# Three seven-product pairs, and pairs with adding DMA, in two recurrent input groups and the first half of an output projection

## The chip, the core and the metric

The kernel runs on one core of a Trainium2 chip. The metric is the device time of one execution in microseconds; the kernel before has a median of 1131.99 us in 3 runs (1131.68 to 1132.94). All times below are microseconds from the start of the profiled span unless marked otherwise. TensorE is called PE, VectorE DVE, ScalarE ACT, GpSimd POOL and SyncE SP, as in the profile.

## The reference

One residual block on 256 tokens of 2048 features, in float32. An input projection feeds an attention half (8 heads) and a recurrent half (8 heads, HGRN2 in chunks of 64); both go through one output projection, and a gated feed-forward follows.

```python
h = rmsnorm(x, norm1_gain[l])
proj = h @ w_in[l]            # q_a k_a v_a | q_r f_r i_r g_r, 1024 columns each
...
attn = rmsnorm(chunk_band_attention(q_a, k_a, v_a, rel_bias[l]), attn_out_gain[l])
rec = hgrn2_mixer(q_r, f_r, i_r, g_r, lb_all[l], grn_norm_gain[l])
# f = lb + (1-lb)*sigmoid(f_raw); k = 1-f; chunkwise recurrence with state
# o = rmsnorm(o) * gain * silu(g_raw)
x = x + concatenate([attn, rec]) @ w_out[l]
ff = silu(h2 @ w_gate[l]) * (h2 @ w_up[l])   # h2 = rmsnorm(x, norm2_gain)
x = x + ff @ w_down[l]
return rmsnorm(x, final_gain)
```

## The kernel before, in words

**Numbers in halves.** Every float32 factor is split into a high part that the array takes whole and a low remainder: ACT copies the high part (a tile named wh, L89) and DVE subtracts it from the raw weights to give the low part (wl, L90). A product is then three matmuls: hi x hi, hi x lo, lo x hi (L336 in the groups that the change touches, L151 and L153 for the transposed projections).

**Groups and pairs.** The columns are worked in groups of 1024 (a `Group`), the 2048-deep contraction in eight pairs of 256 rows. The weights of one pair are one raw tile of 128 x 2048 elements (1 MB), which SP loads (raw, L86) into a ring of three buffers. A pair is one of three kinds. A **d** pair runs 24 matmuls of 128x512 into four accumulators c00, c01, c10, c11; ACT makes two copies of 128x1024 and DVE two splits. An **s** pair forms 2 x 2 blocks as seven products (Strassen's scheme in Winograd's form): 21 matmuls into m1, m5, m6, m7 and three of the c accumulators; for it DVE also makes differences of weight blocks (ta at L385, tb at L386 and L387) and splits those, and the token side needs sums over blocks, made ahead by `row_sums` (tiles wsa and wsb). After the last s pair of a group the products are spread over the outputs. An **a** pair runs 24 matmuls but leaves DVE out: ACT writes the negated high part into a tile named low (L355), POOL issues an adding DMA that reads the same weights from memory a second time and adds them there (L356), and what remains is the low part. `begin` loads the raw of an a pair ahead, `lower` makes half of its low, and `prepare_begun` the high copies; its matmuls are ordered so that those that use low come last. Before, a pairs stand in the second half of the output projection and in the feed-forward.

**What sets the order.** Each engine has an in-order list, made by a scheduler from the program; some instructions are pinned in program order. `run_groups` prepares the next pair while one runs. For an a pair, `begin` and the first `lower` are called in front of the preparation of the pair before it. Between the pairs a number of pieces of the recurrence are taken from a queue (`ticks`), and the last pair of each group is held, so that its matmuls are run by output block together with the next to last.

**Buffers that the steps touch.** The pool of high copies (wh) has four buffers of 128x1024, so that a copy for a pair waits until PE has finished with one of four copies before. The ring of raw has three.

**The stages.** Attention inputs and heads run up to about 197.5; then the group for the recurrent values ("i0", called the value group here), 197.5 to 240; the second pair of transposed recurrent projections, to 291; the gate group ("g0") from 291, with the recurrence of the second four heads woven in; the first half of the output projection (`wout[0]`) from about 338, the second half (`wout[1]`) from about 384; then the feed-forward.

Of the kernel before, what the change touches and what calls it, by code (L numbers as in the profile page):

```python
# [16 lines left out]
P = 128  # L17
S = 256
# [3 lines left out]
W = 512  # L22
# [23 lines left out]
def hybrid_block(ctx: ExitStack, tc: tile.TileContext, x, xT, w_in, w_out, w_gu, w_down,  # L46
                 bias, gains, lbnd, fgain, out):
    nc = tc.nc
# [33 lines left out]
    def dma(o, i):  # L82
        with ExitStack() as st:
            if prev:
                st.enter_context(tc.issue_after(prev[-1]))
            prev.append(nc.sync.dma_start(o, i).ins)  # L86

    def split(hi, lo, src):
        nc.scalar.activation(hi, src, AF.Copy)  # L89
        nc.vector.tensor_tensor(lo, src, hi.bitcast(F32), ALU.subtract)  # L90
# [18 lines left out]
    queue = []  # L109
# [7 lines left out]
    def drain():  # L117
        while queue:
            queue.pop(0)()
# [170 lines left out]
    def row_sums(dst, hi, lo, in_order=False):  # L290
        n = hi.shape[1] // 2
        a = dn.tile([P, 2, 2, S], F32, tag="ta", name="a")[:, 0:n]
        sm = dn.tile([P, 4, 2, P], F32, tag="tb", name="sm")[:, :, 0:n]
        first = nc.vector.tensor_tensor(a, hi.rearrange("p (j k) t -> p j k t", k=2).bitcast(F32),
                                        lo.rearrange("p (j k) t -> p j k t", k=2).bitcast(F32), ALU.add)
        if in_order:
            tc.keep_in_program_order(first)
        a11, a12, a21, a22 = a[:, :, 0, 0:P], a[:, :, 1, 0:P], a[:, :, 0, P:S], a[:, :, 1, P:S]
        nc.vector.tensor_tensor(sm[:, 0], a21, a22, ALU.add)
        nc.vector.tensor_tensor(sm[:, 1], sm[:, 0], a11, ALU.subtract)  # L300
        nc.vector.tensor_tensor(sm[:, 2], a11, a21, ALU.subtract)
        nc.vector.tensor_tensor(sm[:, 3], a12, sm[:, 1], ALU.subtract)
        split(dst[:, 0], dst[:, 1], sm)
# [11 lines left out]
    class Group:  # L315
# [25 lines left out]
            return load_chunk(self.src, self.base + j).rearrange("p (b n) -> p b n", n=W)  # L341

        def begin(self, j):
            raw = own["low"].tile([P, 4, W], F32, name="rawa")
            flat, src = raw.rearrange("p b n -> p (b n)"), self.src[self.base + j]
            if self.src is w_out:
                tc.keep_in_program_order(nc.gpsimd.dma_start(out=flat, in_=src))
            else:
                dma(flat, src)
            self.begun = j, raw, []  # L350

        def lower(self, k):
            j, raw, low = self.begun
            wl = own["low"].tile([P, 2, W], F32R, tag="low", name="low", bufs=3)
            tc.keep_in_program_order(nc.scalar.activation(wl, raw[:, 2 * k:2 * k + 2], AF.Copy, scale=-1.0))  # L355
            nc.gpsimd.dma_start(out=wl.rearrange("p b n -> p (b n)"),  # L356
                                in_=self.src[self.base + j, :, 2 * k * W:2 * (k + 1) * W], accum_op=ALU.add)
            low.append(wl)

        def prepare_begun(self, j):  # L360
            (_, raw, low), self.begun = self.begun, None
            tiles = []
            for k in range(2):
                wh = wsp.tile([P, 2 * W], F32R, tag="wh", name="wh")
                nc.scalar.activation(wh, raw[:, 2 * k:2 * k + 2].rearrange("p b n -> p (b n)"), AF.Copy)
                tiles.append([(wh[:, i * W:(i + 1) * W], low[k][:, i]) for i in range(2)])
# [127 lines left out]
    def att_scores(box, hd, kq, qx, g):  # L494
        h = hd % 4
        sc = paux.tile([P, 384], F32, tag="aux", name="sc")
        nc.tensor.matmul(sc[:, 0:128], lhsT=kq[:, 1, h, :], rhs=kq[:, 0, h, :], start=True, stop=True)  # L497
        kh, kl, qh, ql = kx[:, g, 0, h, :], kx[:, g, 1, h, :], qx[:, 0, h, :], qx[:, 1, h, :]
        nc.tensor.matmul(sc[:, 128:384], lhsT=qh, rhs=kh, start=True, stop=False)
        nc.tensor.matmul(sc[:, 128:384], lhsT=qh, rhs=kl, start=False, stop=False)  # L500
        nc.tensor.matmul(sc[:, 128:384], lhsT=ql, rhs=kh, start=False, stop=True)
        s = box["s"] = abp.tile([P, 384], F32, tag="s", name="s", bufs=2)
        nc.vector.scalar_tensor_tensor(s, sc, ASCALE, G[:, hd, :], ALU.mult, ALU.add)
        nm_ = small.tile([P, 2], F32, tag="nmax", name="nmax")
        sm = small.tile([P, 2], F32, tag="asum", name="asum")
        for t, (a, b) in enumerate(halves):
            nc.vector.tensor_reduce(nm_[:, t:t + 1], s[:, a:b], AX.X, ALU.max, negate=True)
            nc.scalar.activation(s[:, a:b], s[:, a:b], AF.Exp, bias=nm_[:, t:t + 1],
                                 accum_out=sm[:, t:t + 1])
        nc.vector.reciprocal(sm, sm)  # L510
        for t, (a, b) in enumerate(halves):
            nc.vector.tensor_scalar(s[:, a:b], s[:, a:b], sm[:, t:t + 1], None, ALU.mult)

    def att_probs(box):
        pp = paux.tile([P, 384], F32, tag="aux", name="pp")
        for j in range(3):
            nc.tensor.transpose(pp[:, j * P:(j + 1) * P], box["s"][:, j * P:(j + 1) * P], ident)  # L517
        pT = box["pT"] = abp.tile([P, P], F32, tag="pT", name="pT", bufs=2)
        px = box["px"] = abp.tile([P, 2, S], F32R, tag="px", name="px", bufs=2)
        split(px[:, 0, :], px[:, 1, :], pp[:, 0:256])  # L520
        nc.vector.tensor_copy(pT, pp[:, 256:384])

# [52 lines left out]
    def attention_end():  # L575
        def flush(n):
            def run():
                att_values(*ago[n - 2])
                if n - 1 < 8:
                    att_probs(ago[n - 1][0])  # L580
            return run
        queue.append(flush(8))
        queue.append(flush(9))
        queue.append(lambda: att_square(1))
        queue.append(att_rstd)
        for g in range(2):
            for i in range(2):
                queue.append(lambda g=g, i=i: att_norm(g, i))
# [87 lines left out]
    vxs = [abp.tile([P, 2, W], F32R, tag="t4", name="vx", bufs=NT4) for _ in range(2)]  # L676
    v1s = [abp.tile([P, W], F32, tag="ht", name="v1", bufs=3) for _ in range(2)]
    def x_sums(j):
        ks = slice(12 + 2 * j, 14 + 2 * j)
        row_sums(own["wsa"][:, :, :, j:j + 1, :], hx[:, ks, 0, :], hx[:, ks, 1, :])  # L680

    run_groups([Values(0, [("d", j) for j in range(KQ)], w_in, 0, x_pair, None)])
    for g in range(2):
# [15 lines left out]
        if g == 1:  # L699
            queue.insert(0, lambda: att_square(0))  # L700
            dma(lbr.rearrange("p r h -> p (r h)"), lbnd)
            lower_bound()
    attention_end()


    def hgrn_gate(st, g, i):
# [105 lines left out]
        split_scaled(mr[:, 0, ks, tok], mr[:, 1, ks, tok], pt, gg)  # L812

    def xs_of(j, i):
        return own["wsa"][:, 0, i, j - 6, :], own["wsa"][:, 1, i, j - 6, :]
# [66 lines left out]
    mr = mixp.tile([P, 2, 8, S], F32R, tag="mr", name="mr")  # L882
# [37 lines left out]
    class Out(Added):  # L920
# [13 lines left out]
        def between(self, n):  # L934
# [15 lines left out]
    run_groups([gates], wout[0])  # L950
    drain()
    for g in range(2):
        for t in range(NT):
# [274 lines left out]
```

## Time and profile before

| quantity | value |
|---|---|
| median of 3 runs | 1131.99 us (1131.68 to 1132.94) |
| the profiled execution | 1131.58 us |
| span of its trace | 1129.9 us |
| PE busy | 1120.4 us, 99% |
| DVE busy | 990.0 us, 88% |
| ACT busy | 725.3 us, 64% |
| POOL busy | 45.9 us, 4% |
| moved by DMA | 251.05 MB, mean 222 GB/s |

A row of the profile names a line, an engine, an operation and the tiles: `L90 DVE TENSOR_TENSOR wl<-raw,wh 128x1024` is DVE making wl from raw and wh at line 90. In a timeline the first two numbers are the start and the time; `x2` means two operations drawn as one row; a bracket gives the idle time ahead of a row and what ended it. In the chain of waits each row is a stretch of the path that ended last. A row of the stage table gives the stretch, its length and the busy time of PE, its weight loads, DVE, ACT and POOL with counts, the granted clock, the DMA share and GB/s.

### The profile page before, as it was taken

Reading aid. Unit: us, or ns where it says so; the run is one execution under the profiler, and the core shown is the slowest. Engines: PE = TensorE matmul, PEld = TensorE weight load, DVE = VectorE, ACT = ScalarE, POOL = GpSimd, SP = SyncE. Lnnn points to the kernel's source line nnn. Section 1 sums busy time; section 2 is a strip of 40 time slices with the busy share of each in tenths; the row PEclk is TensorE's granted clock in tenths of the full one; section 3 lists DMA queues with packets and bytes.
Section 4 is the critical chain, followed back from the end, with each engine's and each line's share of the span. In section 5 each row is a group of like instructions: output and inputs, shape, how many; then the busy total and the mean of one; then the engine's idle time right before and its main releaser. Section 6 shows DMA issues by size and latency. Waiting matters only on the chain.

```text
span 1129.9 us, 14399 instructions
## 1 busy us (share of the span) xinstructions
PE 1120.4 (99%) x5344; PEld 936.8 (83%) x5344; DVE 990.0 (88%) x1294; ACT 725.3 (64%) x931; POOL 45.9 (4%) x73
## 2 busy tenths in 40 slices
PE   9999999999999999999999999999999999999997
PEld 7888888888888888888888888888888888888885
DVE  7867778996999998789889989989989999899986
ACT  7555656575966666676676676776766565555563
POOL 0000000000000000000000010010010000000000
PEclk9999999999999999999999999999999999999999
DMA  8665544656355768778788878778788756655652
GB/s 335 211 215 190 182 154 149 224 187 259 140 198 183 227 198 324 223 223 228 264 256 236 267 246 248 266 239 253 254 244 249 286 194 219 223 186 187 222 190 108
DMA packets 40246, 251.05 MB, mean 222 GB/s; under 512 B 4592, under 2 KB 5104, under 8 KB 13424
## 3 DMA queue, kind: packets, MB, share of 16 engines
q1 hardware_dynamic: 32832, 220.51, 53.1%
q0 software_dynamic: 7200, 29.36, 13.4%
q8 instruction: 42, 0.69, 0.2%
q10 hardware_dynamic: 144, 0.26, 0.1%
q14 instruction: 28, 0.23, 0.1%
HBM read 245.92 MB, written 4.19 MB: 221 GB/s over the span
## 4 chain that ended last, share of the span: by engine, by line
PE 98%; DVE 1%; ACT 0%; issue 0%; POOL 0%; ACTq 0%; POOLq 0%
PE c L336 62%; PE m L336 16%; PE acc L151 10%; PE acc L153 5%; PE ptr L281 1%; DVE wl L90 0%; PE wm L181 0%; PE po L792 0%; PE pa L765 0%; PE pp L517 0%; ACT wh L89 0%; PE po L794 0%; PE pc L772 0%; PE pa L780 0%; PE sc L497 0%
## 5 line engine op out<-in xcount | busy, mean ns | idle before, releaser
L90 DVE TENSOR_TENSOR wl<-raw,wh 128x1024 fp32r<-128x1024 f32 (+1 forms) x368 | 403.1, 1112 | 60.8 <-ACT wh L89 58.8
L89 ACT ACTIVATE wh<-raw 128x1024 fp32r<-128x1024 f32 (+1 forms) x368 | 351.8, 971 | 157.5 <-PE c L336 78.6
L336 PE MATMUL c<-wh,h 128*128 128x512 f32 x928 | 274.2, 390 | 0.0
L336 PEld LDWEIGHTS c<-wh,h 128*128 128x128 f32 x928 | 174.1, 188 | 36.6 <-DVE ff L1010 0.3
L151 PE MATMUL acc<-hx,wh 128*128 128x512 f32 x512 | 180.0, 395 | 0.0
L153 PE MATMUL acc<-hx,wl 128*128 128x256 f32 x512 | 143.2, 280 | 0.0
L89 ACT ACTIVATE wh<-ta 128x1024 fp32r<-128x1024 f32 x66 | 70.1, 1062 | 88.5 <-PE c L336 44.2
L336 PE MATMUL c<-wl,h 128*128 128x512 f32 x304 | 119.4, 393 | 0.0
L89 ACT ACTIVATE wh<-tb 128x1024 fp32r<-128x1024 f32 x66 | 70.1, 1062 | 69.0 <-PE c L336 36.3
L151 PEld LDWEIGHTS acc<-hx,wh 128*128 128x128 f32 x512 | 96.0, 188 | 21.4
L336 PE MATMUL c<-wh,hx 128*128 128x512 f32 x336 | 105.8, 393 | 0.0
L90 DVE TENSOR_TENSOR wl<-ta,wh 128x1024 fp32r<-128x1024 f32 x66 | 80.7, 1222 | 19.0 <-ACT wh L89 19.0
L153 PEld LDWEIGHTS acc<-hx,wl 128*128 128x128 f32 x512 | 96.5, 189 | 0.1
L90 DVE TENSOR_TENSOR wl<-tb,wh 128x1024 fp32r<-128x1024 f32 x66 | 80.6, 1221 | 12.2 <-ACT wh L89 9.8
L336 PE MATMUL c<-wh,fh 128*128 128x512 f32 x224 | 87.3, 390 | 0.2 <-DVE ff L1002 0.2
L336 PE MATMUL c<-wh,fl 128*128 128x512 f32 x224 | 87.2, 389 | 0.0
L336 PE MATMUL c<-wl,fh 128*128 128x512 f32 x224 | 87.2, 389 | 0.0
L336 PE MATMUL m<-wh,hs 128*128 128x512 f32 x240 | 81.9, 389 | 0.0
L385 DVE TENSOR_TENSOR ta<-raw 128x1024 f32<-128x1024 f32 x66 | 80.6, 1221 | 0.9
L336 PEld LDWEIGHTS c<-wh,hx 128*128 128x128 f32 x336 | 63.3, 189 | 13.7 <-ACT wh L89 0.5
L336 PEld LDWEIGHTS c<-wl,h 128*128 128x128 f32 x304 | 57.1, 188 | 14.1 <-DVE wl L90 2.5
L336 PE MATMUL c<-wl,hx 128*128 128x512 f32 x168 | 65.2, 393 | 0.0
(354 smaller groups left out, 1735.6 us busy)
## 6 DMA issues: line engine op xcount, KB each, us to landing
raw<-in_w_gu_dram SPq DMA_DIRECT2D x68, 1024.0 KB, 7.0
raw<-in_w_in_dram SPq DMA_DIRECT2D x54, 1024.0 KB, 4.8
raw<-in_w_down_dram SPq DMA_DIRECT2D x44, 1024.0 KB, 4.8
rawa<-in_w_gu_dram SPq DMA_DIRECT2D x20, 1024.0 KB, 6.3
low<-in_w_gu_dram POOLq DMA_DIRECT2D x40, 512.0 KB, 6.9
raw<-in_w_out_dram SPq DMA_DIRECT2D x14, 1024.0 KB, 4.9
x<-in_x_dram SPq DMA_DIRECT2D x2, 1024.0 KB, 7.9
rawa<-in_w_out_dram POOLq DMA_DIRECT2D x2, 1024.0 KB, 7.0
```

The costliest lines, as they stand in the source:

```text
L89: nc.scalar.activation(hi, src, AF.Copy)
L90: nc.vector.tensor_tensor(lo, src, hi.bitcast(F32), ALU.subtract)
L151: nc.tensor.matmul(ps[m].rearrange("p j t -> p (j t)"), lhsT=wh[:, col], rhs=both, start=kt == 0, stop=False)
L153: nc.tensor.matmul(ps[m][:, 0, :], lhsT=wl[:, col], rhs=rhs[:, kt, 0, :], start=False, stop=kt == KD - 1)
L281: nc.tensor.transpose(pt[:, j, t, :], nat(t)[:, n0 + j * P:n0 + (j + 1) * P], ident)
L336: nc.tensor.matmul(self.bank[n], lhsT=a, rhs=b, start=self.left[n] == self.total[n], stop=self.left[n] == 1)
L385: nc.vector.tensor_tensor(ta, raw[:, 1:3], raw[:, 0:2], ALU.subtract)
```

## The change

Three tables are changed. The value group and the gate group go from `dddsdsdd` to `dasdssad` (pairs 0, 1, 6, 2, 7, 5, 3, 4 in that order): one d becomes an s, for pair 5, and two d become a, for pairs 1 and 3. The first half of the output projection goes from `ddsdsddd` to `ddsdsasd`: pair 4 becomes s and pair 7 a. Each group then has three s pairs. For pair 5 of the two input groups the token sums are new: they are made once, queued after the attention's setup, into a tile x5 that uses the place of a tile that is now created after the gates. The a pairs of the two input groups load their raw through the common ring of three, and their lows are four tiles of 128x512, each with an adding DMA of 256 KB, in four buffers that they share with the attention's score tile and its split; the score tile and the transposed part of it become one tile for that. The gates' ticks go from {0:2, 1:2, 2:1, 6:2} to {0:2, 1:3, 6:2}.

```diff
         def begin(self, j):
+            if self.src is w_in:
+                self.begun = j, self.load(j), []
+                return
             raw = own["low"].tile([P, 4, W], F32, name="rawa")
...
         def lower(self, k):
             j, raw, low = self.begun
+            if self.src is w_in:
+                low.append([])
+                for b in range(2 * k, 2 * k + 2):
+                    wl = abp.tile([P, W], F32R, tag="bx", name="low", bufs=4)
+                    tc.keep_in_program_order(nc.scalar.activation(wl, raw[:, b], AF.Copy, scale=-1.0))
+                    nc.gpsimd.dma_start(out=wl, in_=self.src[self.base + j, :, b * W:(b + 1) * W], accum_op=ALU.add)
+                    low[k].append(wl)
+                return
...
-        s = box["s"] = abp.tile([P, 384], F32, tag="s", name="s", bufs=2)
+        bx = box["bx"] = abp.tile([P, W], F32, tag="bx", name="bx", bufs=4)
+        s = box["s"] = bx[:, 0:384]
...
-        pT = box["pT"] = abp.tile([P, P], F32, tag="pT", name="pT", bufs=2)
-        px = box["px"] = abp.tile([P, 2, S], F32R, tag="px", name="px", bufs=2)
+        pT = box["pT"] = box["bx"][:, 384:W]
+        px = box["px"] = abp.tile([P, 2, S], F32R, tag="bx", name="px", bufs=4)
...
     def x_sums(j):
+        if j < 0:
+            own["x5"] = mixp.tile([P, 2, 4, 1, P], F32R, tag="mr", name="x5")
         ks = slice(12 + 2 * j, 14 + 2 * j)
-        row_sums(own["wsa"][:, :, :, j:j + 1, :], hx[:, ks, 0, :], hx[:, ks, 1, :])
+        row_sums(own["wsa"][:, :, :, j:j + 1, :] if j >= 0 else own["x5"], hx[:, ks, 0, :], hx[:, ks, 1, :])
...
     attention_end()
+    queue.append(lambda: x_sums(-1))
...
-            items = [(c, int(j)) for c, j in zip("dddsdsdd", "01263745")]
+            items = [(c, int(j)) for c, j in zip("dasdssad", "01627534")]
...
-    gates = Natural("g0", AF.Silu, "gn", {0: 2, 1: 2, 2: 1, 6: 2})
+    gates = Natural("g0", AF.Silu, "gn", {0: 2, 1: 3, 6: 2})
...
-    wout = [Out(0, [(c, int(j)) for c, j in zip("ddsdsddd", "23061745")], w_out, 0, o_of, wsum_of),
+    wout = [Out(0, [(c, int(j)) for c, j in zip("ddsdsasd", "23061745")], w_out, 0, o_of, wsum_of),
```

How the lists of the engines change is seen at three places. The first is ACT at the start of the value group (tb is the copied accumulator of the transposed projection before it, lf and qd are pieces of the recurrence). Before:

```order
L161 COPY tb<-acc 128x256 [waits PE_49]
L89 ACTIVATE wh<-raw 128x1024 [waits PE_49,Activation_49]
L161 COPY tb<-acc 128x256 [waits PE_49]
L757 ACTIVATE qd<-qd 128x512 [waits DVE_49]
L716 ACT_TABLE_LOAD
L716 ACTIVATE lf<-lf 128x512 [waits DVE_49]
```

and now:

```order
L376 ACTIVATE wh<-raw 128x1024 [waits DVE_49,DMAHW7_49,PE_49,Activation_49]
L731 ACT_TABLE_LOAD
L731 ACTIVATE lf<-lf 128x512 [waits DVE_49]
L161 COPY tb<-acc 128x256 [waits PE_49] x2
L361 ACTIVATE low<-raw 128x512 x4
L376 ACTIVATE wh<-raw 128x1024 [waits Activation_49]
L731 ACTIVATE lf<-lf 128x512 [waits DVE_49]
```

The four negated copies of pair 1 stand behind both copies of the last transposed product, and between the two high copies of pair 1.

The second place is DVE in the gate group, from the last splits of the transposed projection on (bb, kdec, kinv, ro are the recurrence). Before:

```order
L385 TENSOR_TENSOR ta<-raw 128x1024
L386 TENSOR_TENSOR tb<-raw,ta 128x512
L387 TENSOR_TENSOR tb<-raw,tb 128x512
L758 TENSOR_TENSOR qd<-qd,eb 128x512
...
L731 TENSOR_TENSOR kdec<-bb 128x1024
L90 TENSOR_TENSOR wl<-raw,wh 128x1024
L725 TENSOR_TENSOR kinv<-kinv,kk 128x1024
L733 TENSOR_TENSOR kdec<-kdec,kk 128x1024
L90 TENSOR_TENSOR wl<-raw,wh 128x512
```

and now, from pair 6's small split on:

```order
L90 TENSOR_TENSOR wl<-raw,wh 128x512
...
L90 TENSOR_TENSOR wl<-raw,wh 128x1024
L90 TENSOR_TENSOR wl<-ta,wh 128x1024
L90 TENSOR_TENSOR wl<-tb,wh 128x1024
L396 TENSOR_TENSOR ta<-raw 128x1024
L746 TENSOR_TENSOR kdec<-bb 128x1024
L740 TENSOR_TENSOR kinv<-kinv,kk 128x1024
L90 TENSOR_TENSOR wl<-raw,wh 128x1024
L748 TENSOR_TENSOR kdec<-kdec,kk 128x1024
L90 TENSOR_TENSOR wl<-raw,wh 128x1024
```

The splits of the first s pair (pair 6) stand ahead of the large pieces of the recurrence, where they stood behind them, and the next s pair's ta (pair 7) stands ahead of the splits of the d pair between them (pair 2).

The third place is ACT late in the first half of the output projection (wsb are sums on the token side, uv the spreading copy after the last s pair's first product). Before:

```order
L355 ACTIVATE low<-rawa 128x1024
L89 ACTIVATE wsb<-sm 128x1024
L417 COPY uv<-m_3369 128x512
L89 ACTIVATE wh<-raw 128x1024 x2
L355 ACTIVATE low<-rawa 128x1024
```

and now:

```order
L89 ACTIVATE wsb<-sm 128x1024
L89 ACTIVATE wh<-ta 128x1024
L428 COPY uv<-m_3423 128x512
L366 ACTIVATE low<-rawa 128x1024
L89 ACTIVATE wh<-tb 128x1024
L89 ACTIVATE wh<-raw 128x1024 x2
L366 ACTIVATE low<-rawa 128x1024
```

The copy of pair 4's tb stands behind the spreading copy and behind the first low of the second half's first pair.

More of the change, by code (lines that the diff above doesn't have):

```diff
@@ L357, in lower @@
                                 in_=self.src[self.base + j, :, 2 * k * W:2 * (k + 1) * W], accum_op=ALU.add)
-            low.append(wl)
+            low.append([wl[:, i] for i in range(2)])
         def prepare_begun(self, j):
@@ L365, in prepare_begun @@
                 nc.scalar.activation(wh, raw[:, 2 * k:2 * k + 2].rearrange("p b n -> p (b n)"), AF.Copy)
-                tiles.append([(wh[:, i * W:(i + 1) * W], low[k][:, i]) for i in range(2)])
+                tiles.append([(wh[:, i * W:(i + 1) * W], low[k][i]) for i in range(2)])
             return [(f"c{t}{h}", self.lhs(2 * j + k, t), tiles[k][h if k == 0 else 1 - h], terms)
@@ L814, in xs_of @@
     def xs_of(j, i):
+        if j == 5:
+            return own["x5"][:, 0, i, 0, :], own["x5"][:, 1, i, 0, :]
         return own["wsa"][:, 0, i, j - 6, :], own["wsa"][:, 1, i, j - 6, :]
@@ L881, in hybrid_block @@
     x2 = res.tile([P, NT, D], F32, tag="res", name="x2")
-    mr = mixp.tile([P, 2, 8, S], F32R, tag="mr", name="mr")
     for t in range(NT):
         dma(x2[:, t, :], x[t])
-    gates = Natural("g0", AF.Silu, "gn", {0: 2, 1: 2, 2: 1, 6: 2})
+    gates = Natural("g0", AF.Silu, "gn", {0: 2, 1: 3, 6: 2})
     for g in range(2):
@@ L945, in between @@
                 second_pair(0)
-    wout = [Out(0, [(c, int(j)) for c, j in zip("ddsdsddd", "23061745")], w_out, 0, o_of, wsum_of),
+    wout = [Out(0, [(c, int(j)) for c, j in zip("ddsdsasd", "23061745")], w_out, 0, o_of, wsum_of),
             Out(1, [(c, int(j)) for c, j in zip("asdsassd", "20316457")], w_out, 8, o_of, wsum_of)]
     run_groups([gates], wout[0])
+    mr = mixp.tile([P, 2, 8, S], F32R, tag="mr", name="mr")
     drain()
```

## The prediction

> **What bounds the kernel now.** I read the summary first, then the chain of waits, then the busy time by stage, and only then the rows of the tiles that the change touches.
>
> ```profile
> PE 1120.4 (99%) x5344; PEld 936.8 (83%) x5344; DVE 990.0 (88%) x1294; ACT 725.3 (64%) x931; POOL 45.9 (4%) x73
> PE 98%; DVE 1%; ACT 0%; issue 0%; POOL 0%; ACTq 0%; POOLq 0%
> 197.57 16.35 PE c L336 x72
> 290.90 16.34 PE c L336 x72
> 319.48 2.29 PE m L336 x9
> 321.77 11.58 PE c L336 x51
> 197.50:240.00 42.50, 42.50 (x190) 35.18 (x189) 39.50 (x46) 28.82 (x33) 0.00 (x0) 1.00 0.58 200
> 291.00:341.00 50.00, 50.00 (x249) 42.17 (x248) 48.72 (x73) 37.38 (x54) 0.00 (x0) 1.00 0.47 169
> 300.60:325.00 24.40, 24.40 (x108) 19.91 (x107) 24.08 (x31) 17.32 (x19) 0.00 (x0) 1.00 0.49 174
> ```
>
> TensorE is the bound everywhere: the chain is 98% PE, and its pieces run back to back (16.35 us for 72 matmuls is 0.227 us each). In the gate group the nine matmuls at 319.48 took 2.29 us where nine times 0.227 are 2.04, so 0.25 us is all that was lost there. The last three rows are stages: first length, then busy time of PE, PE's weight loads, DVE, ACT and POOL, granted clock, DMA share, GB/s. They show the second limit close behind: DVE is busy 39.50 of 42.50 us in the value group, 48.72 of 50 in the gate group, and 24.08 of 24.40 in the middle of the gate group. Matmuls taken away pay only if DVE's and ACT's pieces still come before PE asks for them.
>
> **What is removed.** A d pair is 24 matmuls, a seven-product pair 21, an a pair 24. One pair more is an s pair in each of three groups: 9 matmuls less, 9 x 0.227 = **-2.04 us**, the whole gain on the binding engine. That is 0.18% of the time. Call 0.2% (2.26 us) what a measurement of this kernel can tell from no change: even a change that costs nothing anywhere stays just inside it.
>
> **What is added on DVE and ACT.**
>
> ```profile
> 292.22 1.22 DVE L90 TENSOR_TENSOR wl<-raw,wh 128x1024 fp32r<-128x1024 f32 x1
> 293.35 1.22 DVE L717 TENSOR_TENSOR_SCAN bb<-segm,lf 128x512 f32<-128x512 f32 x1
> 294.49 1.20 DVE L385 TENSOR_TENSOR ta<-raw 128x1024 f32<-128x1024 f32 x1
> 297.15 0.69 DVE L758 TENSOR_TENSOR qd<-qd,eb 128x512 f32<-128x512 f32 x1
> 297.77 0.16 DVE L101 TENSOR_SCALAR ro<-so 128x8 f32<-128x8 f32 x1
> L355 ACT ACTIVATE low<-rawa x44: 1041/1053/1067, 368.8 to 860.4; 128x1024 fp32r<-128x1024 f32 x44
> 52.00:110.00 58.00, 58.00 (x346) 51.38 (x345) 39.53 (x64) 31.35 (x54) 0.69 (x4) 1.00 0.57 200
> ```
>
> By the starts a wide DVE operation occupies 1.13 us (292.22 to 293.35 to 294.49) and a half-wide one 0.61. A d pair costs DVE two wide splits, 2.27 us; an s pair 4 wide and 3 half ones, 6.35 us; an a pair none. Per input group one d becomes s and two d become a: 6.35 - 3 x 2.27 = -0.45 us on DVE, and on ACT eight half-width negated copies of about 0.53 us (half of 1.053) plus about 1.6 us for the s pair, some +6 us. In sum DVE is relieved a little; it is the order that matters. The sums for pair 5 stand early in DVE's order, before the attention heads (stage 52 to 110 has 39.53 of 58 us busy), their last split among the heads; hidden, 0 us, and at most about 0.6 us if the cover were gone. The joined score tile adds no wait ahead of a matmul that was not behind the same matmuls before: 0 us.
>
> **The value group: the first lows.**
>
> ```profile
> 197.26 0.37 ACT L161 COPY tb<-acc 128x256 f32<-128x256 f32 x1 [0.91 <-PE acc L153]
> 457.34 1.04 ACT L355 ACTIVATE low<-rawa 128x1024 fp32r<-128x1024 f32 x1
> 458.81 0.88 POOL L356 DMA_DIRECT2D low<-in_w_gu_dram  x1 [24.33 <-ACT low L355]
> 396.08 1.81 POOL L356 DMA_DIRECT2D low<-in_w_out_dram  x2 [15.13 <-ACT low L355]
> DMA to landing us min/median/max: 5.3/7.0/12.7
> raw<-in_w_in_dram SPq DMA_DIRECT2D x54, 1024.0 KB, 4.8
> ```
>
> ACT is in order, and in the new order the four negated copies stand behind both copies of the last transposed product, which wait for that product's end on PE (197.26). From about 197.9 the copies end at 198.4, 198.9, 199.5 and 200.0. From a copy's end to POOL's issue took about 0.4 us (457.34 + 1.04 to 458.81) and two issues in a row 1.81, 0.93 apart: the issues are at about 198.9, 199.8, 200.8 and 201.7. PE begins the group at 197.34; pair 0 takes 24 x 0.227 = 5.44 us, the sixteen matmuls of pair 1 that need no lows 3.63, so the first low is wanted at 206.4 and, four matmuls on, the fourth-issued low at 207.3. Adding DMAs of 512 KB landed 5.3 us after their issue at best, 7.0 in the median and 12.7 at worst; none of 256 KB is in the trace. Below, half of 5.3, 2.7 us (landing 204.4, no stall); above, 10.2 us, the later of a pair next to a load (211.9, 4.6 us of stall). Two raw loads are issued in the same stretch, so I take the median 7.0: landing 208.7, **+1.4 us**; the group's later s and a pairs I put at 0.1. POOL and DMA carry the wait, and it comes straight on PE, since every matmul in between stands behind it.
> [...]
>
> **The gate group: ACT's list delays DVE.**
>
> ```profile
> 282.66 1.06 ACT L89 ACTIVATE wh<-raw 128x1024 fp32r<-128x1024 f32 x1 [1.78 <-PE acc L151]
> 286.06 1.28 ACT L716 ACT_TABLE_LOAD   x1
> 287.35 0.63 ACT L716 ACTIVATE lf<-lf 128x512 f32<-128x512 f32 x1
> 288.84 0.69 ACT L161 COPY tb<-acc 128x256 f32<-128x256 f32 x2
> 302.24 1.06 ACT L724 ACTIVATE kinv<-bb 128x1024 f32<-128x1024 f32 x1
> 304.15 1.57 ACT L89 ACTIVATE wh<-raw 128x512 fp32r<-128x512 f32 x2
> 309.62 0.42 DVE L741 COPY kf<-kdec 128x512 f32<-128x512 f32 x1
> ```
>
> Before, DVE could fill its time up to 304 with the splits of three d pairs and the recurrence, and the first s pair was wanted only at 307. Now pair 1 gives DVE nothing, and the s pair comes third. On ACT the four copies of pair 1's lows follow the copies of the last transposed product (288.84), with junk, a wide copy, the second log, and an exp table load plus qd (1.28 + 0.54) behind them: about 290 to 296.5. Then come pair 6's first copy, a table load for the root, and the three wide copies, whose buffers come free with pair 0 (296.2) and the two halves of pair 1's hi terms. Worked forward, pair 6's first wide copy ends between 299.3 and 300.6. Until then DVE has nothing left that may run. From there its list has no gap: up to and with the first wide split of pair 5 it holds 14 wide pieces, 8 half ones and three small ones (0.33, 0.33, 0.2): 14 x 1.13 + 8 x 0.61 + 0.87 = 21.6 us. That split is done between 320.9 and 322.2. PE, never stopped, asks for it after 24 + 24 + 21 + 24 + 21 + 7 = 121 matmuls from 290.74, at 318.2. The lateness is 2.7 to 4.0 us; I take **+3.4 us** (DVE from 300.0). It shows as several waits of one to two us on DVE's splits, the largest before the second product of pairs 7 and 5. Bounds: 1.0 if ACT runs 2.4 us ahead of my reckoning, 5.4 if pair 7's raw load also lands late (it is issued behind pair 2's, whose buffer pair 1's raw holds until its second copy; +1.4, since DVE's list is in order). Low waits at pair 1 would come out of the same lateness, not on top: they move PE's later needs back.
>
> **The output projection.**
>
> ```profile
> 352.95 0.67 POOL L347 DMA_DIRECT2D rawa<-in_w_out_dram  x1 [241.77 <-ACT mr L93]
> rawa<-in_w_out_dram POOLq DMA_DIRECT2D x2, 1024.0 KB, 7.0
> 371.44 0.57 ACT L417 COPY uv<-m 128x512 f32<-128x512 f32 x1
> 307.35 1.22 DVE L90 TENSOR_TENSOR wl<-ta,wh 128x1024 fp32r<-128x1024 f32 x1
> ```
>
> The last s pair (4) now stands seventh, and on ACT the spreading copy uv, which waits for the first product of pair 4, and a low copy, which waits for the next added pair's raw, stand ahead of the copy of pair 4's tb. From that pair's start: first product 0.68, uv 0.47, low 1.05, tb's copy 0.96, its split on DVE 1.13: 4.3 us, against 16 matmuls (3.63) to its use: 0.6 us. The raw loads of these pairs are issued by POOL and land 7.0 us later; if that comes late the low copy waits and tb behind it. Above: 2.7 us, with the second low, which is copied about 6 us into the pair, landing 8 to 10 us on. I take **+1.1 us**, lower bound 0.4.
>
> **Sum.** -2.04 + 1.5 + 3.4 + 1.1 = +3.96; on the profiled execution, 1131.58 us, that is 1135.5. The median of the runs before is 1131.99, 0.41 above that execution; on its scale the forecast is **1136.0 us**, 0.35% slower. Its own range, from the three pairs of bounds, not all at an end together: 1133.3 to 1139.5.
>
> **The rivals.**
> *All hidden.* The lows land as fast as half the smallest measured time, and ACT is never the one that DVE waits for. For it: POOL is nearly idle, ACT has 64%, and the gate group lost just 0.25 us before. Against it: 24.08 of 24.40 us of DVE in that group. Time: 1131.99 - 2.04 = 1129.95, no change by the bound, or just faster if the old 0.25 us goes too (1129.7).
> *Only the lows are late.* DVE keeps up, since the a pairs relieve it by 2 x 2.27 us where they stand: -2.04 + 1.5 + 1.1 = +0.56, 1132.5 us, no change. Against it: the relief comes before pair 6, when DVE is short of input, not of time.
> *Raw ring behind the a pairs.* Each input group's a pair holds one of three raw buffers until its second wide copy, so the load after next starts later. If that binds twice, each time by 1.4 us or more, with the lows at the 10.2 us row: -2.04 + 3.0 + 5.4 + 2.7 = +9.1, about 1141 us, slower. It decides from a raw that lands after its pair's ta; the quiet load takes 4.8 us, which speaks against.
>
> **How the numbers follow.** Forecast 0.58, all hidden 0.14, only the lows late 0.18, raw ring 0.10. Of the forecast's range about a tenth lies under 1134.25, where no change ends. Faster: half of all hidden, 0.07. Same: 0.07 + 0.18 + 0.07 = 0.32. Slower: 0.61. The range takes in the first two rivals but the very edge of the hidden one, and most of the slow one: 1130.0 to 1140.5.
>
> **What would show it.** In the changed profile the chain should hold PE waits on DVE's splits between 306 and 323, on pairs 2, 7 and 5, of 2.7 to 4 us in all, with DVE idle for some us between 293 and 300 behind ACT's copies; a PE wait for a low of about 1.4 us near 207; and less than a us near the seventh pair of the first output group. The prediction is wrong if PE's pieces in the gate group still follow each other at 0.227 us, if the 256 KB DMAs land within 5.5 us beside the loads, or if a stall appears in the attention heads or in the second output group, where I put nothing beyond the term above.

## The result and the profile after

The changed kernel takes 1150.88 us (median of 5 runs, 1150.23 to 1154.69) against 1131.99 before: a ratio of 1.0174, 95% interval 1.0163 to 1.0186. Forecast were 1136.0 us in a range of 1130.0 to 1140.5. The direction was right, the size was not: 18.9 us were lost and 4.0 expected.

The page after: busy times, DMA queue of POOL, and the chain by engine.

```profile
PE 1126.4 (98%) x5335; PEld 937.5 (82%) x5335; DVE 994.9 (87%) x1305; ACT 740.7 (65%) x957; POOL 61.6 (5%) x92
...
q0 software_dynamic: 9936, 35.66, 16.3%
...
PE 90%; DMA 4%; DVE 4%; ACT 2%; issue 1%; SPq 0%; ACTq 0%
```

PE has nine matmuls less and yet 6.0 us more busy time, and 4% of the chain is now a DMA, which it never was before. The chain of waits in the two input groups (the pieces between left out) names it:

```profile
199.97 12.42 DMA low<-in_w_in_dram x2
...
231.79 10.14 DMA low<-in_w_in_dram
...
304.09 8.36 DMA low<-in_w_in_dram
...
332.35 9.87 DMA low<-in_w_in_dram
```

Four a pairs, four times the chain runs through the adding DMA of a low: 40.8 us in all. What of it PE could not cover stands in PE's timeline, where the bracket is the idle time ahead:

```profile
208.28 0.96 PE L336 MATMUL c<-low,hx 128*128 128x512 f32 x3 [1.31 <-DMA low<-in_w_in_dram]
212.43 2.07 PE L336 MATMUL c<-low,hx 128*128 128x512 f32 x4 [3.18 <-DMA low<-in_w_in_dram]
...
241.97 1.21 PE L336 MATMUL c<-low,hx 128*128 128x512 f32 x4 [1.77 <-DMA low<-in_w_in_dram]
...
312.49 2.07 PE L336 MATMUL c<-low,hx 128*128 128x512 f32 x4 [2.70 <-DMA low<-in_w_in_dram]
...
342.26 0.97 PE L336 MATMUL c<-low,hx 128*128 128x512 f32 x3 [2.11 <-DMA low<-in_w_in_dram]
```

That is 11.1 us of idle time on PE, and a second loss is in the same rows: four matmuls took 2.07 us at 212.43, where four at full speed take 1.07 (three starts of 0.227 and 0.39 for the last). The stage table shows why (the column behind the busy times is the granted clock):

```profile
197.50:240.00 42.50, 38.01 (x157) 30.06 (x155) 32.04 (x38) 28.69 (x37) 7.13 (x8) 0.92 0.72 206
313.00:317.00 4.00, 4.00 (x13) 3.13 (x12) 2.78 (x4) 2.15 (x4) 0.00 (x0) 0.65 0.34 137
...
206.61:210.03 3.42, 1.32 (x5) 0.48 (x3) 2.97 (x4) 1.06 (x1) 0.00 (x0) 1.00 1.06 231
210.03:213.44 3.41, 1.01 (x2) 0.83 (x3) 1.32 (x2) 0.00 (x0) 0.00 (x0) 0.50 0.82 321
213.44:216.85 3.41, 3.41 (x9) 2.64 (x8) 0.00 (x0) 1.03 (x1) 0.00 (x0) 0.50 0.00 0
...
237.33:240.75 3.42, 2.87 (x13) 2.05 (x11) 3.42 (x4) 3.41 (x4) 0.00 (x0) 1.00 1.05 343
240.75:244.16 3.41, 2.19 (x9) 1.80 (x10) 2.62 (x3) 2.19 (x3) 0.00 (x0) 1.00 0.91 336
244.16:247.57 3.41, 3.41 (x16) 2.82 (x15) 2.29 (x3) 1.45 (x2) 0.00 (x0) 1.00 0.19 79
...
309.01:312.42 3.41, 0.77 (x4) 0.31 (x2) 3.41 (x4) 3.38 (x4) 0.00 (x0) 1.00 1.01 234
312.43:315.84 3.41, 3.35 (x8) 2.68 (x9) 3.32 (x3) 1.59 (x2) 0.00 (x0) 0.50 0.56 231
...
339.73:343.14 3.41, 1.30 (x6) 0.74 (x5) 2.35 (x5) 1.91 (x2) 0.00 (x0) 1.00 0.99 380
343.14:346.56 3.42, 3.42 (x10) 2.65 (x9) 2.22 (x4) 2.43 (x3) 0.00 (x0) 0.50 0.71 223
```

With the waits at 208, 309 and 340 the clock fell to half and a matmul took 0.43 us instead of 0.227 until it came back; with the one at 240 it did not fall. Nine full-length matmuls at 0.43 are 1.8 us more than at 0.227.

Where the clock fell can be read from the traces. In eight of them it fell inside these stages; every stretch at half clock there is 3.41 us long or a whole multiple of it (6.83, 3.41 and 3.41 us in the changed kernel), and in each trace the changes lie whole steps of 3.41 us apart. The last ten rows above are such steps. The falls go with the idle time of PE in the step before. In the step from 206.61, 2.10 us of 3.42 were idle, from two waits together, and the next step ran at half; in the step from 309.01 it was 2.64 us, in the step from 339.73 2.11. The wait at 240 had 1.77 us, but a boundary cut it into 0.55 and 1.22, and the clock held. In the two traces before and after, five of 657 steps at full clock were followed by half clock, two of them at the very end of the programs; PE was idle for 1.92 us or more in these five and for 1.30 or less in the others. Counted over all thirteen traces, it was 30 of some 4270 steps, each with 1.76 us or more of idle PE, and none of the others with more than that. The forecast's wait of 1.4 us lies under every idle time that went with a fall, its upper bound of 4.6 us over the smallest; the prediction did not weigh a change of the clock.

How much each stage lost, from the first matmul of a stage to the first of the next:

| stage | before | after | difference |
|---|---|---|---|
| value group, to the transposed projection | 42.19 | 51.00 | +8.81 |
| gate group, to the output projection | 46.02 | 54.28 | +8.26 |
| output projection, to the feed-forward | 89.44 | 90.62 | +1.18 |
| all else | 952.25 | 952.30 | +0.05 |
| span | 1129.9 | 1148.2 | +18.3 |

With the 0.68 us that each group gains by three matmuls, the value group lost 9.5 us, the gate group 8.9 and the output projection 1.9.

**Why the lows are late.** POOL's timeline after, at the first a pair of each group (x3 are three issues drawn as one row):

```profile
199.26 2.78 POOL L362 DMA_DIRECT2D low<-in_w_in_dram  x3 [88.29 <-DVE tb L162]
204.05 0.88 POOL L362 DMA_DIRECT2D low<-in_w_in_dram  x1 [2.01 <-ACT qd L772]
...
300.00 2.62 POOL L362 DMA_DIRECT2D low<-in_w_in_dram  x3 [67.33 <-PE po L809]
304.09 0.87 POOL L362 DMA_DIRECT2D low<-in_w_in_dram  x1 [1.47 <-DMA low<-in_w_in_dram]
```

and, from the view of the tile over both groups:

```profile
DMA to landing us min/median/max: 3.6/8.0/10.1
```

Three are issued in a row and the fourth some 2 us later; ACT had copied it long before (its four copies ran from 198.28 to 200.49). In all four a pairs the fourth was issued 0.26 to 0.32 us after the first had landed (203.79, 231.47, 303.78 and 332.04), and the program gives it no wait on a DMA of its own four. It then lands 8.3 to 10.1 us after its issue, beside raw loads.

### The profile page after: what moved, and what is told of

It is laid out like the page before. It is cut to its first block, busy times and chain, and to the rows that moved or that the text cites. A ratio compares the mean times of both kernels' runs of the same rounds, so it can differ in the third digit from the quotient of the medians.

```text
span 1148.2 us, 14468 instructions
## 1 busy us (share of the span) xinstructions
PE 1126.4 (98%) x5335; PEld 937.5 (82%) x5335; DVE 994.9 (87%) x1305; ACT 740.7 (65%) x957; POOL 61.6 (5%) x92
## 4 chain that ended last, share of the span: by engine, by line
PE 90%; DMA 4%; DVE 4%; ACT 2%; issue 1%; SPq 0%; ACTq 0%
PE c L336 57%; PE m L336 15%; PE acc L151 9%; PE acc L153 5%; DMA low<-in_w_in_dram 4%; DVE wl L90 1%; PE ptr L281 1%; ACT wh L89 1%; DMA raw<-in_w_in_dram 0%; PE pa L780 0%; PE po L807 0%; DVE at L565 0%; PE pp L529 0%; DVE ma L90 0%; ACT low L361 0%
## 5 line engine op out<-in xcount | busy, mean ns | idle before, releaser
L90 DVE TENSOR_TENSOR wl<-raw,wh 128x512 fp32r<-128x512 f32 (+1 forms) x358 | 390.5, 1107 | 67.9 <-ACT wh L89 65.9
L89 ACT ACTIVATE wh<-raw 128x512 fp32r<-128x512 f32 (+1 forms) x358 | 339.6, 965 | 166.7 <-PE c L336 79.4
L89 ACT ACTIVATE wh<-ta 128x1024 fp32r<-128x1024 f32 x69 | 73.2, 1060 | 82.7 <-PE c L336 42.1
L89 ACT ACTIVATE wh<-tb 128x1024 fp32r<-128x1024 f32 x69 | 73.1, 1060 | 67.8 <-PE c L336 35.4
L90 DVE TENSOR_TENSOR wl<-ta,wh 128x1024 fp32r<-128x1024 f32 x69 | 84.4, 1223 | 18.9 <-ACT wh L89 18.9
L336 PE MATMUL c<-wh,hx 128*128 128x512 f32 x312 | 95.1, 395 | 0.3 <-DVE hx L639 0.2
L90 DVE TENSOR_TENSOR wl<-tb,wh 128x1024 fp32r<-128x1024 f32 x69 | 84.3, 1222 | 11.6 <-ACT wh L89 9.1
L396 DVE TENSOR_TENSOR ta<-raw 128x1024 f32<-128x1024 f32 x69 | 84.3, 1222 | 3.5 <-DMA raw<-in_w_in_dram 1.5
L336 PEld LDWEIGHTS c<-wh,hx 128*128 128x128 f32 x312 | 59.4, 191 | 13.4 <-ACT wh L89 1.0
L367 POOL DMA_DIRECT2D low<-in_w_gu_dram x40 | 34.4, 859 | 393.9 <-ACT low L366 258.9
```

The source lines that it names most:

```text
L336: nc.tensor.matmul(self.bank[n], lhsT=a, rhs=b, start=self.left[n] == self.total[n], stop=self.left[n] == 1)
L367: nc.gpsimd.dma_start(out=wl.rearrange("p b n -> p (b n)"), in_=self.src[self.base + j, :, 2 * k * W:2 * (k + 1) * W], accum_op=ALU.add)
L396: nc.vector.tensor_tensor(ta, raw[:, 1:3], raw[:, 0:2], ALU.subtract)
```

## The experiments

All are edits of the changed kernel. Two explanations stand against each other in the first ones. A: the loss is PE's wait for lows and the half clock that comes with it. B: it is something else, namely the bytes beside the raw loads, DVE's late splits, or the third s pair.

**Two lows of 512 KB instead of four of 256 KB.** The joined score tile is laid out in two tiles of 4 KB for it.

```diff
-                for b in range(2 * k, 2 * k + 2):
-                    wl = abp.tile([P, W], F32R, tag="bx", name="low", bufs=4)
...
+                wl = abp.tile([P, 2, W], F32R, tag="bx" + "ab"[k], name="low", bufs=1)
+                tc.keep_in_program_order(nc.scalar.activation(wl, raw[:, 2 * k:2 * k + 2], AF.Copy, scale=-1.0))
+                nc.gpsimd.dma_start(out=wl.rearrange("p b n -> p (b n)"),
+                                    in_=self.src[self.base + j, :, 2 * k * W:2 * (k + 1) * W], accum_op=ALU.add)
...
```

> The changed kernel with two lows of 128x1024 (adding DMAs of 512 KB) in the two input groups instead of four of 128x512 (256 KB), in the same memory. Theory A (in the changed kernel the fourth adding DMA of each group of four is issued only when the first has landed, 203.79 to 204.05, 231.47 to 231.79, 303.78 to 304.09, 332.04 to 332.35, so no more than three are taken at once): with two there is no hold, the second is issued about 1 us after its copy and the waits for lows shrink from 13 us in all to 4 to 8, with fewer slow-clock stretches behind them; 1140 to 1146 us. Theory B (the bytes beside the raw loads make them late, not the number): as many bytes, so the last low lands as late as before, 1149 to 1153 us.

Measured: 1139.71 us (ratio 1.0069, 1.0054 to 1.0084), 11 us less than the changed kernel with the same bytes. That speaks for theory A, a little below its range. One caveat: the scheduler also moved one of the two copies of the value group's first a pair ahead of the tb copies, so its DMA was issued at 194.77; the second stayed behind them. The largest wait for a low that is left is in the value group (PE's timeline first, then the view of the tile); the clock halved there once more (six matmuls took 2.93 us, where at full clock they take 1.5). It shows the rest of the price, a DMA that takes 10.2 us beside a raw load:

```profile
209.65 2.93 PE L336 MATMUL c<-low,hx 128*128 128x512 f32 x6 [3.20 <-DMA low<-in_w_in_dram]
```

```profile
DMA to landing us min/median/max: 5.3/7.8/10.2
```

**Later low matmuls, first try.**

> The changed kernel with the eight low matmuls of the first a pair of each input group run behind the next s pair instead of ahead of it (4.76 us later on TensorE); nothing else moves on ACT. Theory A (the loss is TensorE waiting for lows, and the clock that drops to half for some 4 us after a wait of over 3 us): the waits at 207 to 212 and at 309 to 312 go to under 1 us each and both slow stretches with them, 6 to 7 us less in the value group and 3 to 5 less in the gate group, where DVE's late splits now show; 1139 to 1143 us. Theory B (DVE's late splits are what sets the end, the low waits only stand where they show first): the waits move to the splits, 1147 to 1152 us.

Measured: 1151.22 us. The edit moved nothing: an a pair's list has 16 entries, eight of them low, and it was cut behind the sixteenth, so the order on every engine was that of the changed kernel. It is a repeat of it (1150.88) and says nothing for either theory.

**The a pairs without the third s pair, and the third s pair without the a pairs.**

```diff
-            items = [(c, int(j)) for c, j in zip("dasdssad", "01627534")]
+            items = [(c, int(j)) for c, j in zip("dasdsdad", "01627534")]   # a pairs alone
+            items = [(c, int(j)) for c, j in zip("ddsdssdd", "01627534")]   # third s pair alone
```

> The changed kernel with the pair 5 of both input groups back to a d pair: the a pairs stay, the third s pairs go there (the output projection stays changed). Theory A (lows and clock): the same waits for lows at the first and the second a pair, 17 us lost against before: 1148 to 1151 us, some 1 us above the changed kernel for the matmuls that come back, less what the s pair cost. Theory B (the third s pair, by DVE's order, as predicted): at most 1 or 2 us beside before, 1131 to 1134 us.

> The changed kernel with the a pairs of both input groups turned into d pairs, the third s pair kept: DVE gets 4.1 us more per group than before, where it had 3.0 us free in the value group and 1.3 in the gate group. Theory A (lows and clock): no waits for lows, TensorE waits for DVE's splits instead, about 1 to 2 us in the value group and 3 to 6 in the gate group, no wait long enough for the clock to drop: 1134 to 1140 us. Theory B (the third s pair by itself is the loss): 1147 us and more.

Measured: 1153.64 us (ratio 1.0197, 1.0172 to 1.0222) with the a pairs alone, 1137.25 us (1.0049, 1.0034 to 1.0064) with the third s pairs alone. The a pairs carry the loss by themselves, a little above what was expected; the run without them is 5.4 us slower than before. This run also keeps the changed order of the pairs, the new ticks and the changed output projection, so the 5.4 us are not the third s pair's alone: 2.9 are in the gate group and 1.4 in the output projection. Without a pairs the value group took 41.56 us, 0.63 less than before, so there the third s pair is free. The gate group took 48.90, 2.88 more. The chain of waits there goes through ACT from 293.21 to 301.19 (loads of function tables, pieces of the recurrence, pair 6's copies; no negated copy is among them), and then through the run of DVE work that the forecast had described, ending at a split for which PE waits:

```profile
293.21 1.28 ACT L772
...
298.63 1.28 ACT L100
...
300.13 1.05 ACT wh L89
...
301.21 2.36 DVE wl L90 x2
303.57 1.14 DVE kdec L746
304.71 1.14 DVE kinv L740
305.84 1.15 DVE wl L90
```

and PE's timeline the three waits, one on a split and two on ACT's copies that come behind it:

```profile
307.03 0.50 PE L336 MATMUL m<-wl,wsa 128*128 128x512 f32 x1 [0.79 <-DVE wl L90]
...
317.10 0.50 PE L336 MATMUL m<-wh,wsa 128*128 128x512 f32 x1 [0.70 <-ACT wh L89]
...
323.83 0.50 PE L336 MATMUL m<-wh,x 128*128 128x512 f32 x1 [0.71 <-ACT wh L89]
```

**Low matmuls after the next pair's, pinned; and the same with two lows.**

```diff
...
-                gr.run(steps)
+                cut = 8 if gr.items[n][0] == "a" and gr.src is w_in else len(steps)
+                own["pin"] = bool(put_off) or cut < len(steps)
+                gr.run(steps[:cut] + put_off)
+                put_off, own["pin"] = steps[cut:], False
...
-                gr.run_blocks(held + steps, gr.block)
+                gr.run_blocks(held + steps + put_off, gr.block)
```

> The changed kernel with the eight low matmuls of each a pair in the two input groups run after the next pair's matmuls (the first a pair: 21 matmuls, 4.76 us later; the second: behind the last pair's, block by block), pinned on TensorE; ACT and POOL keep their order. Theory A (TensorE's waits for lows and the half clock after them are the loss): the first a pair's waits and both slow stretches go, the second's shrink to under 1 us each, DVE's late splits show in the gate group with 2 to 3.5 us; 1134 to 1140 us. Theory B (the lows only stand where DVE's lateness shows first): 1147 to 1152 us.

> Both at once: two lows of 512 KB instead of four of 256 KB in each a pair of the input groups, and their matmuls after the next pair's. Theory A: no wait for a low is left that counts (209.6 landed against about 211 wanted), what stays is DVE's late splits in the gate group, 2 to 3.5 us, and about 1 us in the output projection; 1132 to 1136 us, no change or slightly slower than before. Theory B: 1139 us, as with two lows alone.

Measured: 1139.38 us (ratio 1.0075, 1.0054 to 1.0095) and 1137.89 us (1.0060, 1.0042 to 1.0077). Giving the same DMAs 4.76 us more brings back 11.5 of the 18.9 us, with ACT's and POOL's lists unchanged. DVE's list has five pieces moved, all between 209 and 248 us; in the gate group only PE's order is another, and the group still went from 54.28 to 49.36 us. So most of the loss is the waits for lows, and they are not a mere sign of DVE's lateness. One part of the expectation failed: in the value group a wait for the last low stayed, and the clock halved behind it, with matmuls 0.43 us apart from 215.66 on (PE's timeline):

```profile
214.10 1.33 PE L336 MATMUL c<-low,hx 128*128 128x512 f32 x3 [1.92 <-DMA low<-in_w_in_dram]
```

The two cures hardly add up, and the second run missed its range on the slow side. In its value group a new wait came up; the first row is of DVE's timeline, the second of PE's, the third of the stage table:

```profile
209.75 1.23 DVE L397 TENSOR_TENSOR ta<-raw 128x1024 f32<-128x1024 f32 x1 [2.46 <-DMA raw<-in_w_in_dram]
```

```profile
212.17 0.50 PE L336 MATMUL m<-wl,wsa 128*128 128x512 f32 x1 [1.94 <-DVE wl L90]
```

```profile
213.40:216.40 3.00, 3.00 (x8) 2.35 (x8) 3.00 (x4) 1.06 (x1) 0.00 (x0) 0.50 0.33 63
```

DVE's next piece was the ta of a later s pair, whose raw landed late: the load was issued at 200.18 and took 9.48 us beside the lows, where the median of the 54 such loads before is 4.8; the split that PE wanted stood behind it in DVE's list. PE stood idle 1.94 us, and the clock halved once more. In its gate group DVE waits for ACT's list ahead of pair 6's splits, as the forecast had it (DVE's timeline):

```profile
300.99 0.69 DVE L781 TENSOR_TENSOR qd<-qd,eb 128x512 f32<-128x512 f32 x1 [3.56 <-ACT eb L746]
```

**Eight lows of 128 KB.**

```diff
-                    nc.gpsimd.dma_start(out=wl, in_=self.src[self.base + j, :, b * W:(b + 1) * W], accum_op=ALU.add)
+                    for c in range(2):
+                        lo = b * W + c * W // 2
+                        nc.gpsimd.dma_start(out=wl[:, c * W // 2:(c + 1) * W // 2],
+                                            in_=self.src[self.base + j, :, lo:lo + W // 2], accum_op=ALU.add)
```

> The changed kernel with each adding DMA of 256 KB in the input groups cut in two of 128 KB: eight per a pair, same copies, same bytes. Theory A by number (no more than three adding DMAs are taken at once, whatever their size): the fourth is issued only when the first has landed, the fifth when the second has, and so on; the last low lands 3 to 6 us later than before the cut; 1154 to 1165 us. Theory A by size (it is the bytes in the queue): six are issued in a row, then a hold; last low as now, 1149 to 1153 us. Theory C (no hold by the queue at all, ACT's list just put the fourth there): eight in a row, 1147 to 1152 us.

Measured: 1175.64 us (ratio 1.0386, 1.0368 to 1.0405), further out than the theory by number had it. POOL's timeline at the first a pair:

```profile
198.69 2.79 POOL L364 DMA_DIRECT2D low<-in_w_in_dram  x3 [87.95 <-DVE tb L162]
202.44 0.88 POOL L364 DMA_DIRECT2D low<-in_w_in_dram  x1 [0.95 <-DVE tb L400]
206.40 0.85 POOL L364 DMA_DIRECT2D low<-in_w_in_dram  x1 [3.09 <-ACT wh L89]
209.70 1.72 POOL L364 DMA_DIRECT2D low<-in_w_in_dram  x2 [2.45 <-issue]
213.86 0.88 POOL L364 DMA_DIRECT2D low<-in_w_in_dram  x1 [2.44 <-issue]
```

Again three go at once, now of half the size. The first four landings were at 202.19, 206.15, 209.44 and 209.91 and the fifth at 213.55; the fourth to eighth issue follow these at 202.44, 206.40, 209.70, 210.25 and 213.86. Here too three were in flight, with half the bytes: in these two runs it is the number that stays the same, not the bytes. (The engine named in the brackets is only the one whose signal came last; for the hold itself the program has no signal.)

**Filling the wait with matmuls.**

```diff
+                if n == 1 and gr.items[n][0] == "a" and gr.src is w_in:
...
+                    gr.run(steps[:8])
+                    gr.open("m")
+                    for _ in range(12):
+                        tc.keep_in_program_order(nc.tensor.matmul(
+                            gr.bank["m1"], lhsT=steps[0][1][0], rhs=steps[0][2][0], start=True, stop=True))
+                    gr.run(steps[8:])
...
```

> The changed kernel with twelve more matmuls (2.72 us at full clock, written to the accumulator m1 before it is begun, and overwritten) between the high and the low matmuls of the first a pair of each input group, so that TensorE is busy for part of the time in which it now waits. It leaves nothing out; it adds 24 matmuls. Theory A with the clock (the wait is set by the lows' landing, and the clock halves because TensorE stood idle for over 3 us): the granted clock stays at 1.0 from 213 to 217 and from 313 to 316, the nine and eight matmuls there take 0.227 us again, 3 to 4.5 us less although more is computed; 1146 to 1149 us. Theory D (the slow matmuls have another cause, DMA traffic or the array's reads): no less, 1150 to 1153 us.

Measured: 1150.38 us (ratio 1.0168, 1.0153 to 1.0183), no less than the changed kernel: over the whole a miss. By group it divides. In the gate group the wait shrank to 0.39 us (PE's timeline) and the clock held (stage table):

```profile
314.20 1.19 PE L336 MATMUL c<-low,hx 128*128 128x512 f32 x4 [0.39 <-DMA low<-in_w_in_dram]
```

```profile
313.00:317.00 4.00, 3.61 (x16) 2.69 (x15) 4.00 (x5) 3.16 (x4) 0.00 (x0) 1.00 0.62 239
```

The same stretch had 13 matmuls at a clock of 0.65 in the changed kernel. In the value group the fourth low landed at 213.55 instead of 212.38, a wait with starts 4.29 us apart was left, and the clock fell as before (0.84 granted from 212 to 216, 0.73 from 216 to 220): that group took 52.99 us against 51.00. So the clock held in the one place where the idle time was taken away. DVE's and ACT's lists have pieces moved in this run too, and new waits of up to 0.4 us on ACT's copies came up behind it; that idle time is worth taking away by useless work is not shown.

**The parts alone: the output projection, the third s pair in the value group, and neither table.** The first keeps both input groups as before, the second changes only the value group (`"ddsdssdd"`), the third takes all three tables and the ticks back.

> The output projection's change alone: both input groups and the ticks as before (the joined score tile and the sums for pair 5 stay, though nothing uses the sums). Theory A: what the traces show between the gate group's end and the feed-forward, 93.16 before and 94.33 in the changed kernel, is this part's own: +1.2 us, 1132 to 1134 us. Rival: it is only the input groups' lateness carried on; then 0.68 us is gained by three matmuls less, 1130.5 to 1132 us.

> Only the value group with a third s pair, and with d pairs instead of the a pairs; gate group, ticks and output projection as before. Theory A: with the a pairs and the gate group's change gone nothing is left that loses; three matmuls less, 0.68 us, some 0.4 us given back in the projection behind it, as the run without a pairs showed (41.33 and 49.67 us against 41.96 and 49.24): 1131 to 1132 us, no change that can be measured. Rival (a third s pair costs by itself): 1133 us and more.

> All three tables and the ticks as before; what stays of the change is the joined score tile and the sums for pair 5, which nothing uses. Put at 0 us in the prediction; 1131.3 to 1132.5 us. Rival: the longer hold of the joined tile, or the sums on DVE, delay the attention heads: 1133 us and more.

Measured over 11 runs each: 1133.37 us (ratio 1.0013, 1.0004 to 1.0022), 1132.12 us (1.0002, 0.9993 to 1.0011) and 1132.12 us (1.0000, 0.9991 to 1.0010). The output projection's change costs about 0.9 us by its stage (90.37 against 89.44), mainly in two places, the second in the other half of the projection:

```profile
378.45 0.73 PE L336 MATMUL c<-wh,mr 128*128 128x512 f32 x2 [0.21 <-ACT wh L89]
...
394.20 0.50 PE L336 MATMUL c<-wh,ma 128*128 128x512 f32 x1 [0.52 <-ACT wh L89]
```

The third s pair in the value group gained 0.63 us there (41.55) and gave 0.95 back in the transposed projection behind it (52.01 against 51.06). This trace is of an execution 1.4 us above the median of its 11; in the run without a pairs the same projection gave back 0.43, so the 0.95 may be more than usual. The joined tile and the sums cost nothing. No version tried here is faster than the kernel before.

## Why the prediction was wrong

- **What bounds the kernel, and the gain: right.** PE's pieces are back to back outside the waits, and 0.63 us came out of three matmuls where nothing stood in the way.
- **The value group's lows: the step that failed.** The place, the waiting matmuls and the first issues were right (198.9 forecast, 199.26 measured), and the low DMA took 8.3 us where 7.0 were taken. But the step had POOL issue the fourth low 0.93 us behind the third, at 201.7; it was issued at 204.05, held until the first had landed. The landing was 212.38, outside even the upper bound of 211.9 and 3.7 us behind the 208.7 of the sum: 2.35 from the later issue, 1.3 from the longer DMA. Put at 1.4, the first a pair lost about 7: 4.8 us of added time between starts in the two waits and some 2.2 us at half clock. The trace of before could not show the hold, since nowhere in it do four adding DMAs wait together; still, the bound took for granted that a queue's spacing of two holds for four.
- **The price of a wait: left out.** The sum counted a microsecond of waiting as one. Three of the four a pairs paid 1.7 to 2.2 us more for the clock.
- **"The group's later s and a pairs I put at 0.1": wrong.** The second a pair, whose copies were made in good time, was late all the same (10.14 us from its fourth issue), 1.9 us in the value group; the term of 0.1 had no reason beside it.
- **The gate group: the reason held, but the lows were put at nothing on top of it.** "Low waits at pair 1 would come out of the same lateness" had DVE as the later of the two; the lows were later, and hid DVE's lateness. The two waits for lows added 2.9 and 2.3 us between starts, and the half clock 1.7 each. Where the lows are cured, the forecast's own wait appears. With two lows moved behind, the group loses 2.99 us, with the 0.68 gained 3.7, against 3.4 forecast, and DVE stands idle for 3.56 us behind ACT's list, as described. The places were right in part: PE waits at pair 6 as well, and on ACT's copies as much as on splits. The third s pair alone, with no negated copy on ACT and 4.5 us more splits on DVE, loses 2.88 us. So the negated copies are not needed for a loss of this size, and that the size agrees is partly luck; how much is the third s pair, its earlier place or the new ticks, no run separates.
- **The output projection: about right in size, half in place.** 1.1 forecast; by itself 0.93 + 0.68 = 1.6 lost. The uv, low and tb order cost a wait of 0.4 between starts; the larger one, 0.7, stands in the second half, where nothing was put.
- **The rivals.** The sign of "Raw ring behind the a pairs" came up in one run, DVE held by a late raw for a ta; but that load took 9.48 us instead of 4.8, so its length made it late, and a buffer held longer is not shown. In the same rival's sum the 3.0 is worked out nowhere: by the 10.2 us row that it names, the first lows alone would be 4.6. "All hidden" took 2.7 us for a low of 256 KB; 3.6 at best and 8.0 in the median were measured.

## What to carry to other kernels

A transfer that has been hidden with 18 us of lead (in the feed-forward a low copied at 457.34 was first used at 476.2) says nothing of one with 8: price it by its landing beside the loads it will meet, and count how many of its kind will be in flight at once. Where the bound is TensorE, idle time can cost more than its length: in the changed kernel, where 2.10 to 2.64 us of it gathered in one step of 3.41 us, the half clock behind it added 1.7 to 2.2 us; where a step had 1.22, the clock held. Three waits of 0.70 to 0.79 us, 7 to 10 us apart in the gate group without a pairs, left the granted clock at 1.00 from 291 to 341. And when the whole gain is 0.2%, as here, the order of every engine's list around the edit can outweigh the count of instructions.

## What the runs showed of the hardware

In the changed kernel, with adding DMAs of 256 KB, and in the run with eight of 128 KB, POOL issued three in a row and then held: with 256 KB the fourth went 0.26 to 0.32 us after the first had landed, in all four a pairs; with 128 KB the fourth to eighth of the first a pair went 0.25 to 0.34 us after the landing three before. With 512 KB no more than two were in flight in these groups. All of these DMAs have 128 rows, so whether the hold goes by DMAs or by rows stays open. In the changed kernel a 256 KB adding DMA landed in 3.6 us with no raw load beside it (two more lows were) and, as the fourth of its pair, in 8.3 to 10.1 us beside raw loads. With two lows of 512 KB it was 5.3 us at best and 10.2 at worst, so halving the size did not halve the time here. The clock changed only at whole steps of 3.41 us in these traces: before and after, the five full-clock steps that were followed by half clock had 1.92 us or more of idle PE and the other 652 had 1.30 or less; over all thirteen traces the 30 such steps had 1.76 or more, and no other had more. PE's ends are modelled in the trace, so these figures may be off by a little. How the clock comes back, and why the DMAs beside raw loads take so much longer, stays open.
